# Six two-block sections for the input projection of a decoder layer, five of them with seven products

## The chip, the cores and the metric

The kernel runs on one core of a Trainium2 chip. TensorE multiplies matrices, VectorE (DVE) and ScalarE (ACT) work on tiles, GpSimd (POOL) and SyncE (SP) mostly issue DMAs; each engine takes its instructions in the order in which the program gives them. The metric is the device time in microseconds (us), the median of a few executions. Traces come from one further execution under the hardware profiler, and their times count from the start of its span.

## The reference

One decoder layer on 256 tokens of width 2048, in float32: attention with 16 heads of 128 and a bias table by distance, then a gated feed-forward network of width 5632, each followed by a residual and a layer norm. With 256 tokens there is only one key block, so the attention is plain causal attention. Cut to what is computed:

```python
q, k, v = split(x @ w_qkv, 3)                       # 256 x 2048 each, 16 heads
logits = (q * 128 ** -0.5) @ k.T + bias[t5_bucket(distance)]
p = softmax(where(key <= query, logits, -inf))
x1 = layer_norm(ALPHA * x + (p @ v) @ w_o)
y = layer_norm(ALPHA * x1 + (silu(x1 @ w_gate) * (x1 @ w_up)) @ w_down)
```

## The kernel before

Every large product runs in a split form: a float32 operand is written as a high part `hi` and a remainder `lo` in the format float32r (`split`, L82: a copy on ScalarE, a subtraction on VectorE), and a product takes three matmuls, hi x hi, hi x lo and lo x hi. A matmul has 512 columns and fills one of the eight PSUM banks.

The work is cut into sections (`Sec`, L86), each a few column blocks of 512 of a weight, over eight pairs of 128 input rows. The input projection has four sections q0 to q3, one for each group of four heads, with three column blocks: the group's q, k and v. Then come o0 and o1 (output projection), f0 to f10 (gate and up, one block each) and d (down). `alternate` (L179) lays out two blocks of matmuls for each pair, one for each half of the tokens: 18 matmuls a block in the input projection. The list `blocks` is the order of TensorE's work. Weights of pair p are loaded by SP's queue into one of six raw buffers and split a number of blocks ahead of the pair's first block (`start`, L212 to L221: three, `AHEAD`; in f1 to f10 six or five, `ST_AHEAD`).

The sections f1 to f10 use seven products for eight in the pairs 1, 3 and 5 (`ST`): the two halves of the tokens and the two column blocks form a 2 x 2 scheme over the two rows of a pair, `split_quad` (L240) forms four sums of weights and splits four operands, `combine` (L484) does the same for the input, `half_block` (L278) issues the products into seven banks, and `sums_mid`, `sums_gate` and `sums_up` (L550 to L579) put the results together again.

What else has to be done is hung on a block's number t: `before(t, ...)` ahead of the block's splits, `after(t, ...)` behind its matmuls. The main loop (L695) emits, for each t, the `before` entries, then the splits that are due, then the matmuls, then the `after` entries, and that is the order in every engine's queue. The attention of group g starts behind the first block after section g, one or two steps behind each block (`att_steps`): transposes of q and k of two heads a and b (`at_t1`), scores of a, scores of b with a's normalisation, b's normalisation with the transposes of a's probabilities (`at_t2`), those of b, and the two outputs (`at_o`). `at_s` (L344) also issues the evacuation of the scores on VectorE, the negated maximum `nm` and the exponentials on ScalarE. Banks come from a free list, first in, first out (`bank`, `give`). The second transposed `hn` of section f0 follows two blocks behind it (`gate_t`, L660).

Of the kernel before, what the change touches and what calls it, by code (L numbers as in the profile page):

```python
# [11 lines left out]
F = mybir.dt.float32  # L12
# [15 lines left out]
BIG = -3.0e38  # L28
RL = 384
# [8 lines left out]
ST_FROM = 1  # L38
# [9 lines left out]
def decoder_layer(ctx: ExitStack, tc: tile.TileContext, x, xt, rel_bias, w_qkv, w_o, g1, b1, gb1,  # L48
# [37 lines left out]
    class Sec:  # L86
        def __init__(self, name, chunks, npair, lhs):
            self.name, self.chunks, self.npair, self.lhs = name, chunks, npair, lhs
# [40 lines left out]
    def make_bias():  # L129
        pb = bank("pb")  # L130
        nc.tensor.matmul(pb[:H, :RL], tab, hot, start=True, stop=True)
        rs = const.tile([H, RL], F, name="rs")
        nc.vector.tensor_tensor(rs, pb[:H, :RL], msk, op=OP.add)
        give(pb)
        nc.gpsimd.dma_start(rows, rs)

    def load_bias(g):
# [4 lines left out]
        bias_t[g] = t  # L142

# [11 lines left out]
    x1T, x1D, x1C, x1f = {}, {}, [], {}  # L155
# [14 lines left out]
    FU = [Sec(f"f{i}", [(w_gate, i), (w_up, i)], 8, x1_lhs) for i in range(NF)]  # L170
# [27 lines left out]
    halved = {s.name for s in FU[ST_FROM:]}  # L198
# [72 lines left out]
    def d_lhs(kt):  # L271
        hi, lo = x1D[kt // 8]
        return hi[:, kt % 8, :], lo[:, kt % 8, :]

    def e_lhs(n):
        return x1C[0][:, n, :], x1C[1][:, n, :]

    def half_block(s, p, half):  # L278
        a, b = 2 * p, 2 * p + 1
        if p in ST:  # L280
            w = s.pieces[p, 0]
            n = 2 * ST.index(p)
            lhs = {1: x1_lhs(a, 0), 2: x1_lhs(b, 0), 3: e_lhs(n + 1), 5: e_lhs(n), 7: d_lhs(a),
                   6: d_lhs(b), 4: x1_lhs(b, 1)}
            for n in ((1, 2, 3), (7, 5, 6, 4))[half]:
                product(s, n, lhs[n], w[n], p == ST[-1] and n in (1, 6, 7))
        else:
            hi, lo = s.pieces[p, half]
            for k in range(2):
                kt = a + k  # L290
                w = hi[:, k, :], lo[:, k, :]
                for n, lhs in ((2, x1_lhs(kt, 0)), (4, x1_lhs(kt, 1))) if half == 0 else ((5, x1_lhs(kt, 1)), (3, d_lhs(kt))):
                    product(s, n, lhs, w, p == s.npair - 1 and k == 1)

    def block(s, pairs, m, chunks, ks):
        if s.name in halved:
# [20 lines left out]
    SC = HD ** -0.5  # L317
# [26 lines left out]
    def at_s(h):  # L344
# [139 lines left out]
    def combine(c):  # L484
        if c == 0:
            x1C.extend([p4([P, 8, P], R, "xeh"), p4([P, 8, P], R, "xel")])
        if c % 2 == 0:
            x1D[c // 2] = (p4([P, 8, P], R, "xdh"), p4([P, 8, P], R, "xdl"))
        t0, t1 = (x1f.pop((m, c)) for m in range(2))
        d = s2([P, CW], F, "xd")  # L490
        nc.vector.tensor_tensor(d, t0, t1, op=OP.subtract)
        col = lambda t, k: t[:, k * P:(k + 1) * P]
        for p in (2 * c, 2 * c + 1):
            if p not in ST:
                continue
            a, b = 2 * (p % 2), 2 * (p % 2) + 1
            e = s2([P, 2, P], F, "xe")
            nc.vector.tensor_tensor(col(d, b), col(d, a), col(t1, b), op=OP.add)
            nc.vector.tensor_tensor(e[:, 0, :], col(t1, a), col(t1, b), op=OP.subtract)
            nc.vector.tensor_tensor(e[:, 1, :], col(t0, b), col(d, b), op=OP.subtract)  # L500
            n = 2 * ST.index(p)
            split(x1C[0][:, n:n + 2, :], x1C[1][:, n:n + 2, :], e)
        hi, lo = x1D[c // 2]
# [257 lines left out]
```

## Time and profile before

| | us |
|---|---|
| median of 3 runs | 1125.44 (1125.1 to 1128.34) |
| profiled execution, its own time | 1128.58 |
| its span | 1126.8 |
| TensorE busy | 1108.4 (98%) |
| VectorE busy | 789.2 (70%) |
| ScalarE busy | 552.4 (49%) |
| first matmul of the projection, first of o0 | 4.68, 298.76 |
| DMA | 232.81 MB, mean 207 GB/s |

A busy TensorE is not one at its peak, since the ends of matmuls are modelled and overlap the next; the distance between the starts of two matmuls is their cost. PE is TensorE, PEld its weight loads. "Idle before" names what released an engine after a wait.

### The profile page before, as it was taken

To read this page: it belongs to the slowest core of one execution; us is meant where nothing else is said; L and a number is where in the kernel's file an instruction comes from. 1 tells how busy PE (TensorE), PEld (TensorE's weight loads), DVE (VectorE), ACT (ScalarE), POOL (GpSimd) and SP (SyncE) were. 2 spreads that over 40 slices of the span, in tenths; PEclk is the share of its full clock that TensorE was granted. 3 is DMA by queue.
4 is the path that set the end of the run, shared out by engine and by line. 5 is a ranking of instruction groups with operands and counts; after the bars stand their busy time and mean duration, and the time that the engine had idled before them with its cause. 6 is when DMAs were issued, how large, how long until landed. Compare 5 with 4: busy or idle time off the path is not lost.

```text
span 1126.8 us, 13508 instructions
## 1 busy us (share of the span) xinstructions
PE 1108.4 (98%) x5049; PEld 915.1 (81%) x5049; DVE 789.2 (70%) x1011; ACT 552.4 (49%) x700; POOL 10.3 (1%) x16
## 2 busy tenths in 40 slices
PE   9999999999999999999999999999999999999995
PEld 6888888888888887788888888888888888888884
DVE  7635555564568668888988988988988646664446
ACT  6534444444455456555655655655656534354320
POOL 0000000000000000000000000000000000000001
PEclk9999999999999999899999999999999999999998
DMA  9845555554466636746656646647649584587611
GB/s 330 323 145 175 165 178 185 180 181 154 155 226 200 255 107 219 275 131 236 228 168 240 222 169 244 222 162 251 217 183 339 181 334 184 196 308 261 224 38 75
DMA packets 65890, 232.81 MB, mean 207 GB/s; under 512 B 7520, under 2 KB 7968, under 8 KB 65824
## 3 DMA queue, kind: packets, MB, share of 16 engines
q1 hardware_dynamic: 63344, 223.01, 56.6%
q10 hardware_dynamic: 1872, 6.82, 1.5%
q0 software_dynamic: 608, 2.12, 0.6%
q8 instruction: 39, 0.64, 0.2%
q14 instruction: 27, 0.22, 0.1%
HBM read 222.98 MB, written 8.94 MB: 206 GB/s over the span
## 4 chain that ended last, share of the span: by engine, by line
PE 94%; DVE 3%; ACT 2%; issue 1%; DMA 0%; SPq 0%; POOL 0%; ACTq 0%; POOLq 0%; DVEq 0%
PE acc_f L267 12%; PE acc_f L269 12%; PE acc_f L268 12%; PE acc_q L310 8%; PE acc_q L314 8%; PE acc_q L311 8%; PE acc_d L311 7%; PE acc_d L310 7%; PE acc_d L314 7%; PE acc_o L310 2%; PE acc_o L311 2%; PE acc_o L314 2%; PE ov L396 1%; PE lg L351 1%; PE ht L587 1%
## 5 line engine op out<-in xcount | busy, mean ns | idle before, releaser
L84 DVE TENSOR_TENSOR wl_d<-r_d,wh_d 128x1024 fp32r<-128x1024 f32 x88 | 104.5, 1221 | 72.0 <-ACT wh_d L83 51.9
L310 PE MATMUL acc_q<-wh_q,xh 128*128 128x512 f32 x372 | 148.7, 400 | 0.0
L84 DVE TENSOR_TENSOR wl_f<-r_f,wh_f 128x1024 fp32r<-128x1024 f32 x116 | 135.0, 1218 | 17.5 <-ACT wh_f L83 17.5
L311 PE MATMUL acc_q<-wl_q,xh 128*128 128x512 f32 x372 | 145.3, 391 | 0.0
L310 PE MATMUL acc_d<-wh_d,hh 128*128 128x512 f32 x352 | 137.0, 389 | 0.0
L311 PE MATMUL acc_d<-wl_d,hh 128*128 128x512 f32 x352 | 136.9, 389 | 0.0
L83 ACT ACTIVATE wh_d<-r_d 128x1024 fp32r<-128x1024 f32 x88 | 91.0, 1058 | 76.1 <-DMA r_d<-in_w_down 48.8
L84 DVE TENSOR_TENSOR wl_q<-r_q,wh_q 128x1024 fp32r<-128x1024 f32 x93 | 109.3, 1220 | 26.4 <-ACT wh_q L83 25.7
L83 ACT ACTIVATE wh_f<-r_f 128x1024 fp32r<-128x1024 f32 x116 | 115.7, 1049 | 11.2 <-DMA r_f<-in_w_up 4.5
L267 PE MATMUL acc_f<-wh_f,x1h 128*128 128x512 f32 x300 | 116.8, 389 | 0.0
L269 PE MATMUL acc_f<-wh_f,x1l 128*128 128x512 f32 x300 | 116.7, 389 | 0.0
L268 PE MATMUL acc_f<-wl_f,x1h 128*128 128x512 f32 x300 | 116.7, 389 | 0.0
L314 PE MATMUL acc_q<-wh_q,xl 128*128 128x512 f32 x372 | 105.0, 390 | 0.0
L83 ACT ACTIVATE wh_q<-r_q 128x1024 fp32r<-128x1024 f32 x93 | 93.3, 1053 | 17.2 <-DMA r_q<-in_w_qkv 17.2
L314 PE MATMUL acc_d<-wh_d,hl 128*128 128x512 f32 x352 | 99.9, 389 | 0.0
L314 PEld LDWEIGHTS acc_q<-wh_q,xl 128*128 128x128 f32 x372 | 69.8, 188 | 15.0
L310 PEld LDWEIGHTS acc_q<-wh_q,xh 128*128 128x128 f32 x372 | 70.0, 188 | 14.0 <-issue 0.6
L311 PEld LDWEIGHTS acc_q<-wl_q,xh 128*128 128x128 f32 x372 | 70.0, 188 | 13.2
L83 ACT ACTIVATE aq<-t 128x1024 fp32r<-128x1024 f32 x30 | 31.9, 1063 | 94.7 <-DVE t L247 94.7
L310 PEld LDWEIGHTS acc_d<-wh_d,hh 128*128 128x128 f32 x352 | 66.1, 188 | 13.8
L314 PEld LDWEIGHTS acc_d<-wh_d,hl 128*128 128x128 f32 x352 | 66.1, 188 | 13.7
L311 PEld LDWEIGHTS acc_d<-wl_d,hh 128*128 128x128 f32 x352 | 66.1, 188 | 13.7
(185 smaller groups left out, 1946.5 us busy)
## 6 DMA issues: line engine op xcount, KB each, us to landing
r_q<-in_w_qkv SPq DMA_DIRECT2D x93, 512.0 KB, 4.8
r_f<-in_w_gate SPq DMA_DIRECT2D x88, 512.0 KB, 3.7
r_f<-in_w_up SPq DMA_DIRECT2D x88, 512.0 KB, 5.0
r_d<-in_w_down SPq DMA_DIRECT2D x88, 512.0 KB, 5.9
r_o<-in_w_o SPq DMA_DIRECT2D x32, 512.0 KB, 4.3
hd<-hT ACTq DMA_DIRECT2D x9, 512.0 KB, 6.7
hT<-hd SPq DMA_DIRECT2D x9, 512.0 KB, 3.6
bias<-rows POOLq DMA_DIRECT2D x4, 512.0 KB, 7.4
```

The costliest lines, as they stand in the source:

```text
L83: nc.scalar.activation(hi, src, AF.Copy)
L84: nc.vector.tensor_tensor(lo, src, f32(hi), op=OP.subtract)
L267: nc.tensor.matmul(a, lh, rh, start=start, stop=False)
L268: nc.tensor.matmul(a, lh, rl, start=False, stop=False)
L269: nc.tensor.matmul(a, ll, rh, start=False, stop=stop)
L310: nc.tensor.matmul(a, lh, hi[:, k, :], start=kt == 0, stop=False)
L311: nc.tensor.matmul(a, lh, lo[:, k, :], start=False, stop=False)
L314: nc.tensor.matmul(s.acc[m, c], ll, hi[:, k, :], start=False, stop=kt == nk - 1)
L351: nc.tensor.matmul(b[:, o:o + n], a[:, qs], c[:, ks], start=i == 0, stop=i == 2)
L396: nc.tensor.matmul(b[:, o:o + w], a[:, m, js], c[:, ks:ks + w], start=n == 0, stop=n == 5)
L587: nc.tensor.transpose(out=b[:, j * P:(j + 1) * P], in_=t[:, j * P:(j + 1) * P], identity=ident)
```

## The change

The input projection becomes six sections of two column blocks: q and k of group 0, v of groups 0 and 1, q and k of group 1, q and k of group 2, v of groups 2 and 3, q and k of group 3. All but the first use seven products in the pairs 1, 3 and 5, with the code of the gate/up sections made general; their splits are issued three blocks ahead, those of q0 five. `combine_x` forms the combined input pair by pair behind the blocks of q0. Results are put together in three steps at the end of a section (`sums_1` to `sums_3`), shared with gate/up. Blocks now have 12 matmuls (9 in the first block of a seven-product pair), and seven banks are taken, so attention has one spare.

Attention of groups 0 to 3 runs in q2, q3, q5 and o0. Values stay in float32 and are split per head in `at_t2`; the scale moves into the exponentials; the normalisation moves from VectorE to ScalarE; the outputs of groups 0 to 2 are evacuated unsplit, stored to DRAM, loaded again and split ahead of o0. The second `hn` of f0 is transposed four blocks behind the section instead of two.

```diff
+SC = HD ** -0.5
-ST_FROM = 1
+AHEAD_Q = 5
+QKV = (((0, 0), (1, 0)), ((2, 0), (2, 1)), ((0, 1), (1, 1)), ((0, 2), (1, 2)), ((2, 2), (2, 3)), ((0, 3), (1, 3)))
+SQK, SV = {0: 0, 1: 2, 2: 3, 3: 5}, {1: (0, 1), 4: (2, 3)}
...
-        nc.vector.tensor_tensor(rs, pb[:H, :RL], msk, op=OP.add)
+        nc.vector.scalar_tensor_tensor(rs, pb[:H, :RL], 1.0 / SC, msk, op0=OP.mult, op1=OP.add)
...
+    def combine_x(p):
+        r = x_raw[p]
+        combine(xC, 2 * p, r[:, :, :P], r[:, :, P:], "x")
...
-    Q = [Sec(f"q{g}", [(w_qkv, 4 * i + g) for i in range(3)], 8, x_lhs) for g in range(4)]
+    xC, x1C = {}, {}
+    Q = [Sec(f"q{n}", [(w_qkv, 4 * i + g) for i, g in pair], 8, x_lhs, xC if n else None)
+         for n, pair in enumerate(QKV)]
...
+    for p in range(1, 8):
+        start["q0", p] = first["q0", p] - AHEAD_Q
...
-    for s in FU[ST_FROM:]:
+    for s in [*Q[1:], *FU[1:]]:
         for p in range(s.npair):
-            start[s.name, p] = first[s.name, p] - ST_AHEAD[p in ST]
+            start[s.name, p] = first[s.name, p] - (AHEAD if s in Q else ST_AHEAD[p in ST])
...
+    def combine(comb, kt, t0, t1, name):
+        n = t0.shape[1]
+        d = s2([P, n, P], F, name + "d")
+        nc.vector.tensor_tensor(d, t0, t1, op=OP.subtract)
+        for p in range(kt // 2, (kt + n) // 2):
+            if p not in ST:
+                continue
+            a = 2 * p - kt
+            b = a + 1
+            e = s2([P, 2, P], F, name + "e")
+            nc.vector.tensor_tensor(d[:, b, :], d[:, a, :], t1[:, b, :], op=OP.add)
+            nc.vector.tensor_tensor(e[:, 0, :], t1[:, a, :], t1[:, b, :], op=OP.subtract)
+            nc.vector.tensor_tensor(e[:, 1, :], t0[:, b, :], d[:, b, :], op=OP.subtract)
+            if "e" not in comb:
+                comb["e"] = (p4([P, 8, P], R, name + "eh"), p4([P, 8, P], R, name + "el"))
+            i = 2 * ST.index(p)
+            split(*(v[:, i:i + 2, :] for v in comb["e"]), e)
+        if kt // 8 not in comb:
+            comb[kt // 8] = (p4([P, 8, P], R, name + "dh"), p4([P, 8, P], R, name + "dl"))
+        i = kt % 8
+        split(*(v[:, i:i + n, :] for v in comb[kt // 8]), d)
...
-    def qkv_evac(g, m):
-        s = Q[g]
-        if m == 0:
-            grp[g] = (p4([P, 2, CW], F, f"qn{g}"), p4([P, 2, CW], F, f"kn{g}"),
-                      p4([P, 2, CW], R, f"vh{g}"), p4([P, 2, CW], R, f"vl{g}"))
-        qn, kn, vh, vl = grp[g]
-        nc.scalar.activation(qn[:, m, :], s.acc[m, 0], AF.Copy, scale=SC)
-        nc.vector.tensor_copy(kn[:, m, :], s.acc[m, 1])
-        split(vh[:, m, :], vl[:, m, :], s.acc[m, 2])
-        give(*(s.acc[m, c] for c in range(3)))
+    def new_qk(g):
+        grp[g] = {n: p4([P, 2, CW], F, f"{n}{g}") for n in "qk"}
+        return grp[g]
+    def first_qk(m):
+        t = new_qk(0) if m == 0 else grp[0]
+        nc.scalar.activation(t["q"][:, m, :], Q[0].acc[m, 0], AF.Copy)
+        nc.vector.tensor_copy(t["k"][:, m, :], Q[0].acc[m, 1])
+        give(Q[0].acc[m, 0], Q[0].acc[m, 1])
+    def sums_1(s, t):
+        a = s.acc
+        nc.scalar.activation(t[0], a[1], AF.Copy)
+        nc.vector.tensor_tensor(t[2], t[0], a[6], op=OP.subtract)
+        nc.vector.tensor_tensor(t[3], t[2], a[7], op=OP.add)
+        give(a[1], a[6], a[7])
+    def sums_2(s, t):
+        a = s.acc
+        nc.vector.tensor_tensor(t[0], t[0], a[2], op=OP.add)
+        nc.vector.tensor_tensor(t[1], t[3], a[4], op=OP.add)
+        give(a[2], a[4])
+    def sums_3(s, t):
+        a = s.acc
+        nc.vector.tensor_tensor(t[2], a[5], t[2], op=OP.subtract)
+        nc.vector.tensor_tensor(t[3], a[5], t[3], op=OP.subtract)
+        nc.vector.tensor_tensor(t[2], a[3], t[2], op=OP.add)
+        give(a[5], a[3])
+    sums = {}
+    def qk_sums(g, step):
+        s = Q[SQK[g]]
+        if step == 1:
+            t = new_qk(g)
+            sums[s.name] = [t["q"][:, 0, :], t["q"][:, 1, :], t["k"][:, 0, :], t["k"][:, 1, :]]
+        (sums_1, sums_2, sums_3)[step - 1](s, sums[s.name])
+    def v_sums(n, step):
+        s = Q[n]
+        if step == 1:
+            for g in SV[n]:
+                grp[g, "v"] = p4([P, 2, CW], F, f"v{g}")
+            sums[s.name] = [grp[g, "v"][:, m, :] for g in SV[n] for m in range(2)]
+        (sums_1, sums_2, sums_3)[step - 1](s, sums[s.name])
...
-        nc.vector.tensor_scalar(nm, mx, -1.0, None, op0=OP.mult)
+        nc.vector.tensor_scalar(nm, mx, -SC, None, op0=OP.mult)
...
-        nc.scalar.activation(sc[:, :2 * P], sc[:, :2 * P], AF.Exp, bias=nm[:, 0:1], accum_out=sm[:, 0:1])
-        nc.scalar.activation(sc[:, 2 * P:], sc[:, 2 * P:], AF.Exp, bias=nm[:, 1:2], accum_out=sm[:, 1:2])
+        nc.scalar.activation(sc[:, :2 * P], sc[:, :2 * P], AF.Exp, scale=SC, bias=nm[:, 0:1], accum_out=sm[:, 0:1])
+        nc.scalar.activation(sc[:, 2 * P:], sc[:, 2 * P:], AF.Exp, scale=SC, bias=nm[:, 1:2], accum_out=sm[:, 1:2])
...
-        nc.vector.tensor_scalar(sc[:, :2 * P], sc[:, :2 * P], rs[:, 0:1], None, op0=OP.mult)
-        nc.vector.tensor_scalar(sc[:, 2 * P:], sc[:, 2 * P:], rs[:, 1:2], None, op0=OP.mult)
+        nc.scalar.activation(sc[:, :2 * P], sc[:, :2 * P], AF.Identity, scale=rs[:, 0:1])
+        nc.scalar.activation(sc[:, 2 * P:], sc[:, 2 * P:], AF.Identity, scale=rs[:, 1:2])
...
-        att[h] = [hi, lo]
+        vs = [s2([P, 2, P], R, f"v{i}") for i in "hl"]
+        split(*vs, grp[h // 4, "v"][:, :, h % 4 * P:(h % 4 + 1) * P])
+        att[h] = [hi, lo, *vs]
...
+        if g == 3:
+            oh, ol = oT[g]
+            split(oh[:, j, :], ol[:, j, :], b[:, :S])
+        else:
+            nc.scalar.activation(oT[g][:, j, :], b[:, :S], AF.Copy)
+            if j == 3:
+                nc.scalar.dma_start(od[g], oT.pop(g))
         give(b)
+    def load_o(g):
+        oT[g] = p4([P, 4, S], F, f"o{g}")
+        nc.sync.dma_start(oT[g], od[g])
+    def split_o(g):
+        t = oT[g]
+        oT[g] = (p4([P, 4, S], R, f"oh{g}"), p4([P, 4, S], R, f"ol{g}"))
+        split(*oT[g], t)
...
-    after(6, load_small)
-    after(9, make_bias)
+    after(9, load_small)
+    after(13, make_bias)
+    for p in range(8):
+        after(2 * p + 4, combine_x, p)
+    def at_sums(s, f, *a):
+        t = last[s.name, 1]
+        after(first[s.name, ST[-1]] + 1, f, *a, 1)
+        after(t - 1, f, *a, 2)
+        after(t, f, *a, 3)
+    for m in range(2):
+        after(last["q0", m], first_qk, m)
+    for n in SV:
+        at_sums(Q[n], v_sums, n)
     for g in range(4):
-        after(10 if g < 2 else last[f"q{g - 1}", 1], load_bias, g)
-        for m in range(2):
-            after(last[f"q{g}", m], qkv_evac, g, m)
-        t0 = last[f"q{g}", 1] + 1
+        if g:
+            at_sums(Q[SQK[g]], qk_sums, g)
+        t0 = (first["q2", 0], first["q3", 0], first["q5", 0], first["o0", 0])[g]
+        before(t0 - 3, load_bias, g)
         for n, step in enumerate(att_steps(g)):
             for f, h in step:
                 after(t0 + n, f, h)
+        if g < 3:
+            after(first["o0", 2 * g] - 5, load_o, g)
+            after(first["o0", 2 * g] - 3, split_o, g)
...
-            after(min(t + (m + 1 if i < ST_FROM else 2 + m), first["d", 1]), gate_t, i, m)
+            after(min(t + (2 + m if i else 1 + 3 * m), first["d", 1]), gate_t, i, m)
...
-    for c in range(3):
+    for c in range(2):
...
```

`half_block`, `d_lhs` and `e_lhs` take the section's own operands; otherwise they are as before.

## Rows read from the trace of the kernel before

**Rows 1.** the profile's page, busy time, share and instructions by engine

```profile
PE 1108.4 (98%) x5049; PEld 915.1 (81%) x5049; DVE 789.2 (70%) x1011; ACT 552.4 (49%) x700; POOL 10.3 (1%) x16
```

**Rows 2.** the page, chain that ended last, shares by engine

```profile
PE 94%; DVE 3%; ACT 2%; issue 1%; DMA 0%; SPq 0%; POOL 0%; ACTq 0%; POOLq 0%; DVEq 0%
```

**Rows 3.** two stretches: us, busy (count) by engine, granted clock, DMA, GB/s

```profile
75.00:149.00 74.00, 74.00 (x360) 61.76 (x360) 42.69 (x76) 34.00 (x55) 0.75 (x1) 1.00 0.55 178
487.00:530.00 43.00, 43.00 (x195) 35.62 (x194) 37.37 (x44) 23.45 (x27) 0.00 (x0) 1.00 0.62 210
```

**Rows 4.** timeline, VectorE, behind the first gate/up section: start us, us, what [idle before]

```profile
443.49 0.68 DVE L246 TENSOR_TENSOR t<-r_f,r_f 128x512 f32<-128x512 f32 x1
...
446.02 1.22 DVE L84 TENSOR_TENSOR gq<-r_f,gq 128x1024 fp32r<-128x1024 f32 x1
...
450.03 2.35 DVE L84 TENSOR_TENSOR wl_f<-r_f,wh_f 128x1024 fp32r<-128x1024 f32 x2
452.30 0.68 DVE L544 TENSOR_TENSOR hn<-acc_f,sg 128x512 f32<-128x512 f32 x1
```

**Rows 5.** timeline, TensorE, the same stretch

```profile
449.34 0.39 PE L269 MATMUL acc_f<-wh_f,xdl 128*128 128x512 f32 x1
453.03 1.11 PE L587 MATMUL ht<-ident,hn 128*128 128x128 f32 x4 [3.30 <-DVE hn L544]
453.80 0.78 PE L267 MATMUL acc_f<-gq,x1h 128*128 128x512 f32 x1
...
459.07 0.43 PE L267 MATMUL acc_f<-aq,xeh 128*128 128x512 f32 x1
```

**Rows 6.** stretch behind that wait, columns as in Rows 3

```profile
453.00:456.00 3.00, 2.97 (x9) 2.57 (x10) 2.96 (x5) 1.46 (x2) 0.00 (x0) 0.50 0.84 288
```

**Rows 7.** timeline, TensorE, nine matmuls of section q0

```profile
17.18 0.39 PE L310 MATMUL acc_q<-wh_q,xh 128*128 128x512 f32 x1
...
19.22 0.39 PE L310 MATMUL acc_q<-wh_q,xh 128*128 128x512 f32 x1
```

**Rows 8.** timeline, TensorE, q1: first instruction of attention steps, each behind an 18-matmul block

```profile
83.91 0.38 PE L338 MATMUL t<-ident,qn 128*128 128x128 f32 x2
...
88.46 0.28 PE L351 MATMUL lg<-qkh 128*128 128x256 f32 x1
...
93.27 0.28 PE L351 MATMUL lg<-qkh 128*128 128x256 f32 x1
...
98.09 0.49 PE L379 MATMUL t<-ident,sc 128*128 128x128 f32 x3
102.54 0.49 PE L379 MATMUL t<-ident,sc 128*128 128x128 f32 x3
```

**Rows 9.** groups by line: what, count, busy us, mean ns, idle before

```profile
L84 DVE TENSOR_TENSOR ol<-ov,oh 128x256 fp32r<-128x256 f32 x16 | 6.8, 424 | 29.3 <-ACT oh L83 29.3
L372 DVE TENSOR_SCALAR sc<-sc,rs 128x256 f32<-128x256 f32 x16 | 5.7, 354 | 0.6
```

**Rows 10.** timeline, VectorE, q1: evacuation of two heads' scores

```profile
89.30 0.42 DVE L355 CUSTOM_DVE_ANT_0 sc<-lg,bias 128x256 f32<-128x256 f32 x1 [3.42 <-PE lg L351]
...
95.56 0.42 DVE L355 CUSTOM_DVE_ANT_0 sc<-lg,bias 128x256 f32<-128x256 f32 x1
...
96.23 0.17 DVE L361 TENSOR_SCALAR nm<-mx 128x2 f32<-128x2 f32 x1
```

**Rows 11.** timeline, ScalarE, q1: one head's exponentials

```profile
96.43 0.51 ACT L363 ACTIVATE sc<-sc,nm 128x256 f32<-128x256 f32 x1 [2.42 <-DVE nm L361]
...
96.94 0.39 ACT L364 ACTIVATE sc<-sc,nm 128x128 f32<-128x128 f32 x1
97.23 0.19 ACT L364 ACTIVATION_READ_ACCUMULATOR sc<-sc,nm 128x1 f32 x1
```

**Rows 12.** the page, DMA issues: count, KB each, us to landing

```profile
hd<-hT ACTq DMA_DIRECT2D x9, 512.0 KB, 6.7
...
bias<-rows POOLq DMA_DIRECT2D x4, 512.0 KB, 7.4
```

More of the change, by code (lines that the diff above doesn't have):

```diff
@@ L86, in decoder_layer, with __init__ @@
     class Sec:
[L87 to L88 removed]
+        def __init__(self, name, chunks, npair, lhs, comb=None):
+            self.name, self.chunks, self.npair, self.lhs, self.comb = name, chunks, npair, lhs, comb
             self.acc = {}
@@ L269, in product, with d_lhs, e_lhs @@
         nc.tensor.matmul(a, ll, rh, start=False, stop=stop)
[L271 to L276, printed above, removed]
+    def combine(comb, kt, t0, t1, name):
[19 more added lines that the diff above has]
+        split(*(v[:, i:i + n, :] for v in comb[kt // 8]), d)
+    def d_lhs(s, kt):
+        return tuple(v[:, kt % 8, :] for v in s.comb[kt // 8])
+    def e_lhs(s, n):
+        return tuple(v[:, n, :] for v in s.comb["e"])
     def half_block(s, p, half):
@@ L291, in half_block @@
                 w = hi[:, k, :], lo[:, k, :]
-                for n, lhs in ((2, x1_lhs(kt, 0)), (4, x1_lhs(kt, 1))) if half == 0 else ((5, x1_lhs(kt, 1)), (3, d_lhs(kt))):
+                for n, lhs in ((2, s.lhs(kt, 0)), (4, s.lhs(kt, 1))) if half == 0 else ((5, s.lhs(kt, 1)), (3, d_lhs(s, kt))):
                     product(s, n, lhs, w, p == s.npair - 1 and k == 1)
     def block(s, pairs, m, chunks, ks):
-        if s.name in halved:
+        if s.comb is not None:
             half_block(s, pairs[0], m)
@@ L395, in at_o @@
             for a, c in ((vh, hi), (vh, lo), (vl, hi)):
-                nc.tensor.matmul(b[:, o:o + w], a[:, m, js], c[:, ks:ks + w], start=n == 0, stop=n == 5)
+                nc.tensor.matmul(b[:, o:o + w], a[:, m, :], c[:, ks:ks + w], start=n == 0, stop=n == 5)
                 n += 1
-        oh, ol = oT[g]
-        split(oh[:, j, :], ol[:, j, :], b[:, :S])
-        give(b)
+        if g == 3:
[5 more added lines that the diff above has]
+                nc.scalar.dma_start(od[g], oT.pop(g))
+        give(b)
+    def load_o(g):
[5 more added lines that the diff above has]
+        split(*oT[g], t)
     def att_steps(g):
@@ L482, in ln1_t, with combine_x1 @@
         split(hi[:, a:a + 4, :], lo[:, a:a + 4, :], t.rearrange("p (j c) -> p j c", j=4))
[L484 to L503, printed above, removed]
-        n = 4 * (c % 2)
-        split(hi[:, n:n + 4, :], lo[:, n:n + 4, :], d.rearrange("p (j c) -> p j c", j=4))
+    def combine_x1(c):
+        t0, t1 = (x1f.pop((m, c)).rearrange("p (j c) -> p j c", j=4) for m in range(2))
+        combine(x1C, 4 * c, t0, t1, "x1")
     def ln1_affine(m, c):
@@ L640, in decoder_layer @@
     for c in range(4):
-        after(f0_t[1][0] + (1, 2, 4, 6)[c], combine, c)
+        after(f0_t[1][0] + (1, 2, 4, 6)[c], combine_x1, c)
     after(f0_t[0][3], store_y, 0)
@@ L655, in decoder_layer @@
         else:
-            after(first[f"f{i}", ST[-1]] + 1, sums_mid, i)
-            after(t - 1, sums_gate, i)
-            after(t, sums_up, i)
+            at_sums(FU[i], gate_sums, i)
         for m in range(2):
-            after(min(t + (m + 1 if i < ST_FROM else 2 + m), first["d", 1]), gate_t, i, m)
+            after(min(t + (2 + m if i else 1 + 3 * m), first["d", 1]), gate_t, i, m)
     after(dn_t[0][0] - 10, load_ln, g2, b2, "ln2")
@@ L685, in decoder_layer @@
         load_x(0, slice(k, k + 1))
-        for c in range(3):
+        for c in range(2):
             r, src = s.raws[0, c]
@@ L690, in decoder_layer @@
         split_x(0, slice(k, k + 1))
-        for c in range(3):
+        for c in range(2):
             hi, lo = s.pieces[0, c]
@@ L702, in decoder_layer @@
                 split_x(p, slice(0, 2))
-            if ss.name in halved and p in ST:
+            if ss.comb is not None and p in ST:
                 split_quad(ss, p)
```

63 lines of the change are left out of this document (22 added, 41 removed).

## The prediction

> **What bounds the kernel now.** I read the engine shares first, then the chain of waits, then the busy time by stretch. TensorE is busy 98% of the span [rows 1] and carries 94% of the chain that ended last [rows 2], so a matmul removed is time removed as long as TensorE stays fed. VectorE is the next engine: 42.69 of 74 us in an attention section of the input projection, 37.37 of 43 us in a section of the gate/up stage, which already works with seven products [rows 3]. TensorE was busy throughout both stretches. So VectorE at 87% of a stretch does no harm by itself; the order of its queue has to be looked at as well.
>
> One place shows that. Behind the first gate/up section, the second `hn` (L544) waits on VectorE behind the seven-product split of the next section and a plain split: the seven-product split runs from 443.49 to 450.03 (6.54 us), the plain one to 452.30 (2.27 us), and only then does `hn` start [rows 4]. TensorE's last matmul before the wait starts at 449.34; the transposes of `hn` start at 453.03 [rows 5]. With 0.23 us for that last matmul TensorE stood for 3.46 us. Behind the wait the granted clock is 0.50 (1.2 of 2.4 GHz) [rows 6]; twelve matmuls take from 453.80 to 459.07 [rows 5].
>
> **What is removed.** Nine matmuls start between 17.18 and 19.22 [rows 7]: 0.2267 us each. A seven-product pair needs 21 matmuls for 24. Five sections with three such pairs: 45 fewer, 45 x 0.2267 = 10.2 us. All are on the path.
>
> The Trainium skill ("TensorE: Matmul & The Clock Gate", Back-to-back issue gap) gives about 131 ns for a sustained matmul of 512 columns; by it the edit would save 5.9 us, and the sum below would be 4.3 us higher. The pitch of this kernel's own matmuls is 227 ns, so I go by that.
>
> The second `hn` transposes move from two blocks behind the first gate/up section to four. The wait of 3.46 us goes, and with it the slow clock: twelve matmuls at full pitch are 2.72 us instead of 5.27, and four transposes 0.47 [rows 8] instead of 0.77; together 2.9. What is late next: in block 3 of that section product 7 takes the seventh bank of the free list, which is one that the same `hn` reads until 452.98 [rows 4]. Block 3 would start at 449.57 + 9 x 0.2267 = 451.6, so 1.4 us remain. Gain 3.46 + 2.9 - 1.4 = 5.0 us (between 0, if the short wait also lowers the clock and costs what the long one did, and 6.4).
>
> **What VectorE gets.** Fifteen seven-product splits for plain ones: 15 x (6.54 - 2.27) = 64 us. Sums: 7 x 0.63 (four adds from 443.49 to 446.02 [rows 4]) = 4.4 us in each of five sections, 22 us, where about 9 us of evacuation go. Values split per head: 16 x 0.42 [rows 9] = 7 us. Combining `x`: 16 such operations and a few small ones, 11 us. The two normalising operations, 0.35 and about 0.28, leave for ScalarE: -10 us [rows 9]. Net about 83 us over the projection, nearly all in five sections. An attention section then has 3 x 6.54 + 5 x 2.27 + 4.4 + about 12 = 47 us of VectorE against 183 x 0.2267 + 9.2 = 50.7 us of TensorE (9.2: four heads at 0.47, 0.73, 0.37 and 0.73, each the distance of two rows less the 4.08 of 18 matmuls [rows 8]). By the average it fits; sections q1 and q4, without attention, have 35 against 41.5 and I cost them at nothing: nothing in them waits for TensorE before block 11, so VectorE runs ahead.
>
> **Where the order bites.** Splits are issued three blocks ahead, so pair 3's seven-product split stands in VectorE's queue between head a's scores (behind block 2) and head b's scores and a's normalisation (behind block 3); the transposes of a's probabilities come behind block 4. From the first score matmul of a: score evacuation starts after 0.84 us and takes 0.84 to the end of `nm` [rows 8, 10], 1.7; split 6.54, 8.2; b's scores 0.84, 9.0. ScalarE then does b's exponentials, 0.99 from 96.43 to 97.42 [rows 11], 10.0, and only then a's normalisation, priced by the same two tiles there, 0.42 + 0.39, 10.8. TensorE arrives after 0.73 + 2.72 (block 3) + 0.73 + 2.72 (block 4) = 6.9 us. It waits **3.9 us**. In the kernel before, the same place held a plain split, blocks took 4.08 us and a's normalisation did not follow b's exponentials, and a's transposes (98.09) came 4.82 us behind b's scores (93.27) [rows 8], that is one block and the scores themselves, with no wait.
>
> In q2 and q5 VectorE is late before that. From the end of the last block but one of the section before: two sums 1.2, split of pair 1 6.5, three sums 1.8, a's q and k 0.6, plain split 2.3, b's q and k 0.6, with 0.2 to start: 13.2 us. TensorE has finished a's scores after 2.72 + 2.72 + 0.47 + 2.72 + 0.47 + 2.04 + 0.73 = 11.9. So 1.3 more: **5.2 us** in each. In q3 the heads' q and k are q2's own sums, which stand behind q3's pair 1: 0.2 + 1.2 + 6.54 + 1.8 = 9.75 us against 0.73 + 2.72 + 0.73 + 2.72 = 6.9: **2.9 us** at the first transposes, then 3.9. The second pair of heads meets plain splits there, and waits under 0.2 us. Together 5.2 + 2.9 + 3.9 + 5.2 = **17.2 us** (bounds: 0, if something starts these splits earlier; 22, if each normalisation and each transition is 1 us later).
>
> Three of the four waits are longer than the 3.46 us after which the clock is seen to fall: 3 x 2.9 = **8.7 us**. The fourth I count at nothing (0 to 2.9). The Trainium skill (same page, Part 1) reports 6 to 14 slow matmuls for one kernel from run to run; at 0.21 us each, three falls would by that cost 3.8 to 8.8 us. Here twelve were slow.
>
> **Costed at nothing.** ScalarE's extra splits, exponent scale and normalisations: it is busy 34 of 74 us [rows 3]; the order effect is counted above. Combining `x` lies beside q0's blocks, which wait for no such operation before q1; if it were in the way, the first section would lose up to its 11 us. The spill of three outputs: a store lands 6.7 us after its issue [rows 12]; the reload of group 2 stops SP's queue until then, with the pieces for o0's pair 4 behind it, whose use is 13 us further on. The bias load on POOL's queue is issued five blocks (13.6 us) ahead of use and lands in 7.4 [rows 12]. Four chunks instead of six before the first matmuls: 0, within 1 either way. One spare bank: its turns wait for the same VectorE operations as counted.
>
> **The sum.** -10.2 - 5.0 + 17.2 + 8.7 = +10.7 us. The profiled execution took 1128.58 us (span 1126.8), so 1139.3 for such a one. It lies 3.1 above the median of the three runs, 1125.44, and the new time is a median too: **1136 us**.
>
> **Rivals.** (A) VectorE keeps up: the splits start early enough that nothing waits. For: 47 against 50.7 us, and gate/up sections at 87% without waits. Against: head a's scores stand before the split, so it can't start before TensorE is through block 2; the gate/up sections issue six blocks ahead, these three. Then only the gains count, 1125.4 - 15.2 = 1110: faster. (B) The waits come, but the clock stays up or the waits shrink by as much: 1125.4 + 17.2 - 15.2 = 1127.4, the same. For: the only fall seen had transposes around it; against: rows 6. (C) More of it: the fourth wait lowers the clock too and the mended place gains nothing: 1136 + 2.9 + 5.0 = 1144. The point that decides between A and the forecast is whether a's probabilities are normalised within 6.9 us of a's scores.
>
> **How the numbers follow.** The forecast 0.54, C 0.08, B 0.2, A 0.18 (which may end anywhere from 1110 to 1121, as part of the waits stays). About 0.3% (3.4 us) is what a measurement can tell here. Faster 0.18, same 0.2, slower 0.62. The forecast's own range is 1130 to 1142; to leave out no more than 2 in 10, the range goes from 1117, inside A, to 1144.
>
> **What would show it.** Right: in q2, q3 and q5 TensorE idle for 4 to 5 us in front of the first probability transposes, released by ScalarE's normalisation, with VectorE busy on a seven-product split just before; one wait of about 3 us at the start of q3's attention on VectorE's sums; granted clock 0.50 behind them; no 3.46 us wait behind the first gate/up section. Wrong: the projection from first matmul to o0 in 284 us or less with TensorE unbroken (A), or waits with matmuls still 0.23 us apart behind them (B).

## The result and the profile after

The changed kernel takes **1145.48 us** (1144.72 to 1146.3, 4 runs) against 1125.27 for the kernel before beside it: ratio 1.0174, 95% interval 1.0154 to 1.0194, slower by some 20 us. The forecast was 1136, slower by some 11, and its range ended at 1144: the side was right, the forecast size was half of the measured one, and the time lies 1.5 us above the range. The profiled execution took 1146.3 (span 1144.5), 17.7 more than the profiled one of before.

From the page of after, busy time by engine and the chain that ended last, the lines that answer to [rows 1] and [rows 2]:

```profile
PE 1105.3 (97%) x5004; PEld 908.7 (79%) x5004; DVE 867.8 (76%) x1124; ACT 591.5 (52%) x782; POOL 10.3 (1%) x16
PE 82%; DVE 10%; ACT 4%; issue 2%; DMA 1%; SPq 0%; POOL 0%; ACTq 0%; DVEq 0%; POOLq 0%
```

The 45 matmuls are gone, but TensorE's part of the chain fell from 94% to 82%: VectorE and ScalarE now decide 14% of the way.

The first matmul of each stage shows where the time went. From the first matmul of the projection to that of o0 it is 313.3 us (before 294.1), +19.2; o0 and o1 take 99.2, +1.8; gate/up takes 474.8, -3.5; the rest is within 0.3. The answer to [rows 3], two stretches of after (columns as there):

```profile
118.00:160.00 42.00, 37.23 (x186) 30.58 (x185) 30.94 (x52) 21.26 (x39) 0.76 (x1) 0.98 0.47 156
500.00:540.00 40.00, 40.00 (x182) 33.09 (x181) 35.76 (x42) 23.27 (x27) 0.00 (x0) 1.00 0.62 208
```

In the attention section TensorE idles for nearly 5 of 42 us although VectorE is busy for only 31 of them; in the gate/up stage VectorE is busier and TensorE never stops.

TensorE's waits in after, grouped by what ended them (total us, times, longest us):

```profile
PE t L447 <- ACT sc L441: 16.9, 6, 4.3
PE t L406 <- DVE k L379: 4.7, 2, 3.9
PE ht L631 <- ACT hT L632: 2.5, 1, 2.5
```

L447 transposes the probabilities, L441 is the normalisation on ScalarE, L406 transposes q and k, L379 is the last of the sums. A row shows some 0.16 us less than TensorE stood, as the last matmul's modelled end lies behind its pitch of 0.23; below, waits are counted from that pitch. In the projection they are 4.45 (q2), 1.66, 4.07 and 3.84 (q3), 1.72, 4.43 (q5) and 1.73: 21.9 us. The first one, TensorE in q2:

```profile
109.35 0.39 PE L280 MATMUL acc_q<-wh_q,xl 128*128 128x512 f32 x1
114.03 0.90 PE L447 MATMUL t<-ident,sc 128*128 128x128 f32 x3 [4.29 <-ACT sc L441]
114.58 0.77 PE L278 MATMUL acc_q<-wh_q,xh 128*128 128x512 f32 x1
...
118.99 0.55 PE L279 MATMUL acc_q<-wl_q,xdh 128*128 128x512 f32 x1
```

VectorE and ScalarE in the same stretch:

```profile
110.29 1.22 DVE L87 TENSOR_TENSOR bq<-t,bq 128x1024 fp32r<-128x1024 f32 x1
111.42 0.42 DVE L423 CUSTOM_DVE_ANT_0 sc<-lg,bias 128x256 f32<-128x256 f32 x1
```
```profile
112.30 0.51 ACT L431 ACTIVATE sc<-sc,nm 128x256 f32<-128x256 f32 x1 [2.94 <-DVE nm L429]
...
113.59 0.39 ACT L441 ACTIVATE sc<-sc,rs 128x128 f32<-128x128 f32 x1
```

The last piece of the seven-product split, then b's scores, b's exponentials, then a's normalisation, and only then the transposes: the forecast's chain, step by step. Behind the wait the matmuls stand 0.43 us apart instead of 0.23, at this granted clock (columns as in [rows 3], the clock behind the busy times):

```profile
114.00:118.00 4.00, 3.97 (x11) 3.29 (x12) 2.15 (x4) 3.35 (x6) 0.00 (x0) 0.50 0.01 4
```

That is half of the 2.4 GHz level. Behind the four long waits of the projection 11, 6, 11 and 7 matmuls are slow and lose 7.5 us together; behind the three short ones none is. So the projection's 19.2 us are -10.2 (matmuls) + 21.9 (waits) + 7.5 (clock). The start and the slow transposes, each under 2 us, are not separated, so it is partly luck that the sum closes exactly.

### The profile page after: what moved, and what is told of

Read it like the earlier page. It is cut to its first block, busy times and chain, and to the rows that moved or that the text cites. A ratio compares the mean times of both kernels' runs of the same rounds, so it can differ in the third digit from the quotient of the medians.

```text
span 1144.5 us, 13666 instructions
## 1 busy us (share of the span) xinstructions
PE 1105.3 (97%) x5004; PEld 908.7 (79%) x5004; DVE 867.8 (76%) x1124; ACT 591.5 (52%) x782; POOL 10.3 (1%) x16
## 4 chain that ended last, share of the span: by engine, by line
PE 82%; DVE 10%; ACT 4%; issue 2%; DMA 1%; SPq 0%; POOL 0%; ACTq 0%; DVEq 0%; POOLq 0%
PE acc_f L278 12%; PE acc_f L280 12%; PE acc_f L279 12%; PE acc_d L342 7%; PE acc_d L343 7%; PE acc_d L346 7%; PE acc_q L278 4%; PE acc_q L280 4%; PE acc_q L279 4%; PE acc_o L342 2%; PE acc_o L343 2%; PE acc_o L346 2%; PE acc_q L343 1%; PE acc_q L346 1%; PE acc_q L342 1%
## 5 line engine op out<-in xcount | busy, mean ns | idle before, releaser
L86 ACT ACTIVATE aq<-t 128x1024 fp32r<-128x1024 f32 x45 | 47.7, 1060 | 124.5 <-DVE t L258 114.6
L87 DVE TENSOR_TENSOR wl_q<-r_q,wh_q 128x1024 fp32r<-128x1024 f32 x64 | 75.6, 1221 | 12.4 <-ACT wh_q L86 11.9
L86 ACT ACTIVATE wh_q<-r_q 128x1024 fp32r<-128x1024 f32 x64 | 64.1, 1048 | 3.3 <-DMA r_q<-in_w_qkv 2.9
L280 PEld LDWEIGHTS acc_f<-wh_f,x1l 128*128 128x128 f32 x300 | 56.3, 188 | 11.8
L278 PEld LDWEIGHTS acc_f<-wh_f,x1h 128*128 128x128 f32 x300 | 56.3, 188 | 11.6
L279 PEld LDWEIGHTS acc_f<-wl_f,x1h 128*128 128x128 f32 x300 | 56.3, 188 | 11.6
L278 PE MATMUL acc_q<-wh_q,xh 128*128 128x512 f32 x150 | 62.7, 418 | 0.0
L280 PE MATMUL acc_q<-wh_q,xl 128*128 128x512 f32 x150 | 60.2, 401 | 0.0
L279 PE MATMUL acc_q<-wl_q,xh 128*128 128x512 f32 x150 | 59.9, 399 | 0.0
```

Source lines behind the costliest of these rows:

```text
L86: nc.scalar.activation(hi, src, AF.Copy)
L87: nc.vector.tensor_tensor(lo, src, f32(hi), op=OP.subtract)
L278: nc.tensor.matmul(a, lh, rh, start=start, stop=False)
L279: nc.tensor.matmul(a, lh, rl, start=False, stop=False)
L280: nc.tensor.matmul(a, ll, rh, start=False, stop=stop)
```

## Experiments

The leading theory (ORDER): the waits come from what stands ahead in the queues of VectorE and ScalarE. The rival (VOLUME): VectorE has too much to do. All edits are against the changed kernel unless another is named, all ratios against the kernel before on the same chip.

### 1. The attention of the first three groups one block later

```diff
-                after(t0 + n, f, h)
+                after(t0 + n + (g < 3), f, h)
```

> The changed kernel with the attention of groups 0 to 2 one block later against the splits, nothing else. Theory ORDER (TensorE waits because attention operations stand behind a split in the queues of VectorE and ScalarE): the seven-product split of pair 3 then stands before head a's scores instead of behind them; the first waits shrink from 4.3 to about 1.7 us, the second ones (1.7) go, the wait on q3's sums falls from 4.1 to about 1, and no wait is long enough for the slow clock: 1123 us, between 1119 and 1129. Rival VOLUME (VectorE has too much work in an attention section, 47 of 51 us): the work is the same, 1142 to 1147 us.

Measured 1146.96 (1144.9 to 1148.12), ratio 1.0195 (1.0180 to 1.0210): nothing gained, and inside VOLUME's range, not ORDER's. TensorE in q2:

```profile
110.58 0.43 PE L419 MATMUL lg<-qkh 128*128 128x256 f32 x1 [2.45 <-DVE mx L425]
...
120.11 0.55 PE L447 MATMUL t<-ident,sc 128*128 128x128 f32 x3 [1.85 <-DVE ptl L87]
```

The one long wait became two short ones: b's score matmuls wait for the one spare bank, which a's evacuation (L425), now behind the split, still holds, and a later step meets the next split. The waits moved with the order, but the time didn't: with seven-product splits this frequent, a shift by a block only moves the collision. By the time alone this run speaks for VOLUME; it is experiment 3 that parts the two.

### 2. a's normalisation right behind a's scores

```diff
-            one = [[(at_t1, a)], [(at_t1, b)], [(at_s, a)], [(at_s, b), (at_n, a)],
+            one = [[(at_t1, a)], [(at_t1, b)], [(at_s, a), (at_n, a)], [(at_s, b)],
```

> The changed kernel with the normalisation of head a issued right behind its own scores instead of behind head b's. It is then done before the transposes need it. If the place of the normalisation alone makes the wait, the six waits in front of probability transposes go, and with them the slow clock: 1121 to 1126 us. If the one spare bank is as late (head b's scores are evacuated behind the split too), the first waits stay at 3.5 to 4 us and the second ones at about 1: 1141 us, 1137 to 1144.

Measured 1145.22 (1144.97 to 1145.27), ratio 1.0181 (1.0166 to 1.0196). TensorE, then VectorE in q2:

```profile
113.12 0.52 PE L447 MATMUL t<-ident,sc 128*128 128x128 f32 x3 [3.91 <-DVE mx L425]
```
```profile
111.20 1.22 DVE L87 TENSOR_TENSOR bq<-t,bq 128x1024 fp32r<-128x1024 f32 x1
112.34 0.42 DVE L423 CUSTOM_DVE_ANT_0 sc<-lg,bias 128x256 f32<-128x256 f32 x1
```

a is normalised long before (by 106.8 us), and the wait stays: its releaser is now the evacuation of b's scores, whose bank the transposes need. So the place of the normalisation alone was not the point that decides; the spare bank behind the split is as late. The time lies 1.2 us above the range put for this; in the second pairs the transposes of b's probabilities now wait too, 1.1 us three times.

### 3. The normalisation back on VectorE

```diff
-        nc.scalar.activation(sc[:, :2 * P], sc[:, :2 * P], AF.Identity, scale=rs[:, 0:1])
+        nc.vector.tensor_scalar(sc[:, :2 * P], sc[:, :2 * P], rs[:, 0:1], None, op0=OP.mult)
```

(and the same for the second part)

> The changed kernel with the normalisation back on VectorE. ORDER: a's normalisation no longer stands behind b's exponentials on ScalarE, each of the six waits gets about 0.85 us shorter: 1139 us, 1136 to 1142. VOLUME: VectorE gets 10 us more work, so 1147 to 1155 us.

Measured **1134.46** (1134.38 to 1135.6), ratio 1.0085 (1.0069 to 1.0102): 11 us faster with more on VectorE. That refutes VOLUME as it was put. ORDER's 1139 was 4.5 us too high: the waits before the probability transposes shrank by the 0.85 us each that it counted, and beside them the wait on q3's sums fell from 4.07 to 2.98 and o0's loss of 1.8 went. TensorE in q2, first and second pair of heads:

```profile
112.26 0.90 PE L447 MATMUL t<-ident,sc 128*128 128x128 f32 x3 [3.45 <-DVE sc L441]
139.51 0.55 PE L447 MATMUL t<-ident,sc 128*128 128x128 f32 x3 [0.65 <-DVE sc L441]
```

The waits are 4.29 and 1.50 in after. On ScalarE a's normalisation comes behind b's exponentials; on VectorE it runs beside them.

### 4. Seven products in two pairs instead of three in q2, q3 and q5

```diff
+            self.st = (1, 5) if name in ("q2", "q3", "q5") else ST
-        if p in ST:
+        if p in s.st:
```

Pair 3 is then formed from an operand that is not the plain difference, so the sums of these sections differ; the work is that of a plain pair.

> The changed kernel with seven products in pairs 1 and 5 only in q2, q3 and q5 (nine matmuls more, 2.0 us). ORDER: a plain split stands in the critical place, the first waits fall from 4.3 to about 1.7 us like the second ones, and the slow clock behind them goes: 1132 us, 1128 to 1136. VOLUME: 13 us less for VectorE, which would give at most those 13 us less the 2: 1134 to 1140. A weak separation; it prices the pair.

Measured 1138.69 (1137.87 to 1140.1), ratio 1.0125 (1.0109 to 1.0140). That is inside VOLUME's range and 2.7 us above ORDER's, whose centre was 6 us too low; the run does not speak against VOLUME. The first pair of heads in q2 and q5 still waits 2.28, the sums 4.06, and the clock falls behind both kinds. Counted by the trace: 9 matmuls +2.0, waits -6.5, slow matmuls -1.9 make -6.4; measured -6.8 (-7.6 between the profiled executions).

### 5. The seven-product split in two parts, a block apart

```diff
-        split(*a2, t13)
-        split(*b2, t24)
+        def rest():
...
+            split(*a2, t13)
+            split(*b2, t24)
+        rest() if late is None else before(late, rest)
```

> The changed kernel with each seven-product split of the projection issued in two parts, one block apart (two adds and three operands first, then two adds and the other operands); the same instructions, 3.0 and 3.5 us of VectorE instead of 6.5 in one piece. ORDER: b's scores and a's normalisation no longer stand behind 6.5 us, the first waits fall from 4.3 to about 0.5, the wait on q3's sums from 4.1 to nothing, the slow clock goes, the second waits (1.7) stay: 1122 us, 1118 to 1130. VOLUME: the same work and the same waits in other places, as it was when attention was moved by one block: 1142 to 1147 us.

Measured 1139.54 (1138.36 to 1140.03), ratio 1.0123 (1.0109 to 1.0137). TensorE in q2:

```profile
110.62 0.55 PE L454 MATMUL t<-ident,sc 128*128 128x128 f32 x3 [1.75 <-ACT sc L448]
116.10 0.55 PE L454 MATMUL t<-ident,sc 128*128 128x128 f32 x3 [2.19 <-DVE ptl L87]
```

The wait on q3's sums is down to 0.5, and a's wait nearly to what the second pair has (1.7); but b's transposes now meet the other half. The time lies between the two ranges: ORDER's size was wrong again.

### 6. Experiments 3 and 5 together, with two steps more

Beside both edits, a's transposes go ahead of b's normalisation, and the second `hn` transposes five blocks behind f0:

```diff
-            after(min(t + (2 + m if i else 1 + 3 * m), first["d", 1]), gate_t, i, m)
+            after(min(t + (2 + m if i else 1 + 4 * m), first["d", 1]), gate_t, i, m)
```

> As the run with two parts, with the normalisation on VectorE, a's transposes in front of b's normalisation, and the second hn of the first gate/up section transposed five blocks behind it. ORDER: the second waits fall to 0.8, the 3.1 us in front of hn go: 1114 us, 1110 to 1120, faster than both kernels. VOLUME: 10 us more for VectorE, 1130 to 1140 us, not below the kernel before.

Measured 1127.83 (1126.05 to 1129.6, 10 runs), ratio 1.0021 (1.0012 to 1.0030). That is 14 us above ORDER's 1114, though below VOLUME's range. No wait is left behind f0, but eleven in the projection are, 0.7 to 2.3 us each, 14 us together.

### 7. No seven products in the projection

Six plain sections (45 matmuls back), with four spare banks instead of one:

```diff
-    Q = [Sec(f"q{n}", [(w_qkv, 4 * i + g) for i, g in pair], 8, x_lhs, xC if n else None)
+    Q = [Sec(f"q{n}", [(w_qkv, 4 * i + g) for i, g in pair], 8, x_lhs)
```

> The changed kernel without the seven products in the projection (six plain sections of two blocks, four spare banks, no combining of x). 45 matmuls more, 10.2 us. If only the seven-product splits make the waits: no wait left, 1122 to 1127 us. If blocks of 2.72 us instead of 4.08 are themselves too short for the chain of scores, exponentials, a plain split, scores, exponentials and normalisation: all six pairs of heads wait 1.7 us as the second pairs do, 1135 us, 1131 to 1139.

Measured 1134.87 (1133.86 to 1135.26), ratio 1.0082 (1.0068 to 1.0095). TensorE in q2:

```profile
113.70 0.55 PE L456 MATMUL t<-ident,sc 128*128 128x128 f32 x3 [1.50 <-ACT sc L450]
```

There are six such waits, 1.65 or 1.72 each, with no seven-product split in the projection: some 10 us come from the two-column sections and the place of the normalisation, as the second reading had it. The fifteen seven-product pairs as placed, with the three banks that they take, make it 10.6 us worse, though they save 10.2 of matmuls.

### 8. The kernel before, with the later hn alone

```diff
-            after(min(t + (m + 1 if i < ST_FROM else 2 + m), first["d", 1]), gate_t, i, m)
+            after(min(t + (1 + 3 * m if i < ST_FROM else 2 + m), first["d", 1]), gate_t, i, m)
```

> The kernel before with the second hn of the first gate/up section transposed four blocks behind it instead of two, nothing else. By the stage of the two traces (478.2 and 474.8 us) the edit saves 3.5 us where the clock falls behind the old wait. If the clock falls there in some runs of the kernel before and not in others (its runs lie near 1125 and near 1128): 1124 to 1125 us, with the spread gone. If it falls in all: 1122 us.

Measured 1124.78 (1122.92 to 1125.4, 11 runs), ratio 0.9989 (0.9980 to 0.9998). The edit is worth 0.6 us in the median; no run came near 1128, but the runs lie near 1123.3 and near 1125.1, so a spread remains. It goes with the granted clock: its mean over the span is 0.996 in the runs near 1123.3 and 0.994 or 0.995 in the others. The trace still has a wait of 2.67 us before the second `hn` transposes, with slow matmuls behind it; why the mean clock differs from run to run stays open.

### 9. Seven products only in q1 and q4, where no attention runs

Plain sections as in experiment 7 for the others, with the normalisation on VectorE and `hn` five blocks behind f0:

```diff
-    Q = [Sec(f"q{n}", [(w_qkv, 4 * i + g) for i, g in pair], 8, x_lhs, xC if n else None)
+    Q = [Sec(f"q{n}", [(w_qkv, 4 * i + g) for i, g in pair], 8, x_lhs, xC if n in SV else None)
```

> Seven products stay only in q1 and q4, the two sections that no attention runs beside; q0, q2, q3 and q5 are plain sections of two column blocks. Besides, the normalisation is back on VectorE and the second hn of the first gate/up section is transposed five blocks behind it. Counted from the form without seven products in the projection (1134.87): 18 matmuls fewer, 18 x 0.2267 = -4.1; the 2.5 us wait behind the first gate/up section goes; six waits on the normalisation shrink from 1.5 to 0.65, -5.1. ORDER theory (a seven-product split costs only where attention steps stand behind it in VectorE's queue): 1123 us (1120 to 1127), TensorE unbroken through q1 and q4. Rival VOLUME (each seven-product pair costs VectorE time that is missing later, as the 15 pairs cost 10.6 us net): 6 x 0.7 = +4.2 instead of -4.1, 1131 us (1128 to 1134), with waits at the starts of q2 and q5.

Measured **1122.29** (1121.73 to 1122.93, 8 runs), ratio 0.9977 (0.9967 to 0.9987): where ORDER put it. TensorE waits six times on the normalisation, 0.89 us each (0.74 in the rows), and nowhere in q1 or q4.

### 10 and 11. An extra block before a's probabilities, with and without those pairs

Both against experiment 9; the second is without seven products in q1 and q4 too.

```diff
-            one = [[(at_t1, a)], [(at_t1, b)], [(at_s, a)], [(at_s, b), (at_n, a)],
-                   [(at_n, b), (at_t2, a)], [(at_t2, b)], [(at_o, a)], [(at_o, b)]]
+            one = [[(at_t1, a), (at_t1, b)], [(at_s, a)], [(at_s, b)], [(at_n, a)],
+                   [(at_t2, a), (at_n, b)], [(at_t2, b)], [(at_o, a)], [(at_o, b)]]
```

> As the kernel with seven products in q1 and q4 alone, and the attention steps spaced anew: both heads' q and k are transposed behind one block, and one block more stands between the scores of head b and the transposes of a's probabilities. ORDER theory (the 0.65 us left before a's probability transposes is the chain scores, plain split, normalisation against two 2.72 us blocks): with a third block that wait goes everywhere, -0.7 x 6 = 4 us against that kernel: 1119 us (1116 to 1123). Rival (what is gained there is lost at the front: with both transposes behind one block, head a's score matmuls come behind VectorE's plain split, 2.3, and two operand splits in less than 3.2 us): waits of 0.5 to 1 us at the first score matmuls instead, time as without the edit, 1123 us (1121 to 1126).

> No seven products in the projection at all, with the other three edits of the kernel with the spaced steps (normalisation on VectorE, second hn five blocks behind, the extra block before a's probabilities). What it tells: what the six seven-product pairs of q1 and q4 are worth by themselves. ORDER: they are worth their 18 matmuls, so this kernel is 4.1 us slower than the one with them, 1123 us (1120 to 1127). Rival VOLUME: they cost as much as they save or more, so this one is as fast or up to 4 us faster.

Measured 1122.38 (1122.06 to 1122.58, 11 runs; ratio 0.9977, 0.9968 to 0.9986) and 1126.59 (1125.48 to 1127.22, 11 runs; ratio 1.0011, 1.0002 to 1.0020). The difference, 4.2 us, is the 18 matmuls (4.1): the pairs in q1 and q4 are worth all that they save. The extra block gained nothing, and not for the rival's reason either, since no score matmul waits. Experiment 10 in q2, second pair of heads, TensorE, then VectorE, then ScalarE:

```profile
137.91 0.52 PE L447 MATMUL t<-ident,sc 128*128 128x128 f32 x3 [0.79 <-DVE sc L441]
```
```profile
134.54 2.36 DVE L87 TENSOR_TENSOR wl_q<-r_q,wh_q 128x1024 fp32r<-128x1024 f32 x2 [2.06 <-ACT wh_q L86]
136.82 0.16 DVE L438 TENSOR_SCALAR rs<-sm 128x2 f32<-128x2 f32 x1
...
137.49 0.28 DVE L441 TENSOR_SCALAR sc<-sc,rs 128x128 f32<-128x128 f32 x1
```
```profile
132.57 0.51 ACT L431 ACTIVATE sc<-sc,nm 128x256 f32<-128x256 f32 x1 [1.97 <-DVE nm L429]
...
133.46 1.99 ACT L86 ACTIVATE wh_q<-r_q 128x1024 fp32r<-128x1024 f32 x2
```

The normalisation stands behind a plain split whose VectorE half is idle for 2.06 us, because its ScalarE half is queued behind b's exponentials. The operands of the normalisation had been ready all that time: a's exponentials end at 130.6 us.

### 12. Both normalisations ahead of that split

Against experiment 10:

```diff
-            one = [[(at_t1, a), (at_t1, b)], [(at_s, a)], [(at_s, b)], [(at_n, a)],
-                   [(at_t2, a), (at_n, b)], [(at_t2, b)], [(at_o, a)], [(at_o, b)]]
+            one = [[(at_t1, a), (at_t1, b)], [(at_s, a)], [(at_s, b), (at_n, a), (at_n, b)], [(at_t2, a)],
+                   [(at_t2, b)], [(at_o, a)], [(at_o, b)], []]
```

> As the kernel with seven products in q1 and q4 alone, with another order of the attention steps: both heads' q and k are transposed behind one block, the scores of a one block later, then, behind the same block, the scores of b and both heads' normalisations, and a block later each the transposes of the probabilities. ORDER theory (what was left of the waits, 0.75 us six times, was a normalisation behind a plain split whose VectorE half stands idle, 2.06 us from 132.48 to 134.54 in the kernel with the extra block, because its ScalarE half is queued behind the exponentials): with the normalisations ahead of that split they run inside its idle time, nothing waits, and six waits of 0.75 us go: 1122.3 - 4.5 = 1118 us (1116 to 1120). Rival (the waits aren't on the path, since TensorE makes them up at the next bank or transfer): 1122 us (1121 to 1123). Second rival (b's normalisation, which needs b's exponentials, holds up the split behind it, and product blocks wait for weights): 1122 to 1126 us.

Measured **1116.45** (1116.17 to 1117.06, 5 runs), ratio 0.9924 (0.9910 to 0.9937): faster than both kernels. The page's busy time and chain, then TensorE in q2 at the second pair of heads, and VectorE there:

```profile
PE 1099.6 (99%) x5031; PEld 908.7 (82%) x5031; DVE 830.5 (75%) x1087; ACT 567.4 (51%) x735; POOL 10.3 (1%) x16
PE 94%; DVE 2%; ACT 1%; DMA 1%; issue 1%; SPq 0%; POOL 0%; ACTq 0%; POOLq 0%; DVEq 0%
```
```profile
133.16 0.49 PE L447 MATMUL t<-ident,sc 128*128 128x128 f32 x3
```
```profile
131.96 0.28 DVE L441 TENSOR_SCALAR sc<-sc,rs 128x128 f32<-128x128 f32 x1
...
133.18 0.28 DVE L441 TENSOR_SCALAR sc<-sc,rs 128x128 f32<-128x128 f32 x1
133.46 2.36 DVE L87 TENSOR_TENSOR wl_q<-r_q,wh_q 128x1024 fp32r<-128x1024 f32 x2
```

Both normalisations run in what was the idle time, and no wait of TensorE over 0.2 us is left in q1 to o1, although a's transposes come a block earlier behind b's scores than in experiment 10: the order gained what the distance had not. Against the profiled execution of before, gate/up is 6.2 us shorter, about what the wait and the low clock behind f0 took [rows 5, 6], and the projection 5.8, of which 4.1 are the 18 matmuls; that execution lay 3.1 above the median of its kernel, so the medians differ by less, 8.7. TensorE does 27 matmuls more than in after, and the kernel is 29 us faster.

## Why the prediction was half right

The mechanism held at the first pairs of heads and at q3's sums; the sum came out 9.5 us low, by the terms below.

**The matmuls, -10.2**, and **the waits of the first pair of heads** held: mechanism, place and releaser as put; 4.45, 3.84 and 4.43 us against 5.2, 3.9 and 5.2.

**The second pair of heads, "waits under 0.2 us there": the step that failed most.** It waits 1.66, 1.72 and 1.73, 5.1 us in all. VectorE, then ScalarE, then TensorE in after:

```profile
138.31 2.36 DVE L87 TENSOR_TENSOR wl_q<-r_q,wh_q 128x1024 fp32r<-128x1024 f32 x2 [2.00 <-ACT wh_q L86]
140.59 0.42 DVE L423 CUSTOM_DVE_ANT_0 sc<-lg,bias 128x256 f32<-128x256 f32 x1
```
```profile
137.24 2.00 ACT L86 ACTIVATE wh_q<-r_q 128x1024 fp32r<-128x1024 f32 x2
...
142.76 0.39 ACT L441 ACTIVATE sc<-sc,rs 128x128 f32<-128x128 f32 x1
```
```profile
143.20 0.55 PE L447 MATMUL t<-ident,sc 128*128 128x128 f32 x3 [1.50 <-ACT sc L441]
```

I had priced a plain split at its 2.27 us of VectorE. It costs 4.3, as its first half waits on ScalarE behind the exponentials that follow a's scores. The chain comes to 8.6 us against 6.9 on TensorE. In the kernel before, that hop stood in the trace too, but a block took 4.08 us:

```profile
92.15 3.50 DVE L84 TENSOR_TENSOR wl_q<-r_q,wh_q 128x1024 fp32r<-128x1024 f32 x3 [2.00 <-ACT wh_q L83]
```

Experiments 3, 7 and 12 show what makes this wait: with the normalisation on VectorE 0.81 remain (0.65 in the row), without seven products in the projection nothing changes, and with the order of experiment 12 all of it goes.

**The sums of q3, 2.9**: 4.07. What delayed the second pair also held back what stands ahead of them: the first step of q2's sums found VectorE idle behind a copy that follows a's normalisation on ScalarE.

```profile
143.66 0.69 DVE L365 TENSOR_TENSOR k<-q,acc_q 128x512 f32<-128x512 f32 x1 [1.96 <-ACT q L364]
```

With the normalisation on VectorE (experiment 3) it is 2.98, as forecast.

**The low clock, 8.7**: 7.5. It fell behind all four long waits, also the one that I had counted at nothing, but over 6 to 11 matmuls, not twelve each time. The Trainium skill ("TensorE: Matmul & The Clock Gate", Part 1) reports 6, 11 or 14 slow matmuls at the start of one kernel from run to run; here, behind waits in the middle of one execution, there were 11, 6, 11 and 7.

**The hn behind f0, -5.0**: -3.5. The bank that I named as late next did not hold up product 7. Another did: the second transposes take the bank of the first, whose evacuation stands on ScalarE behind the next split's copies. TensorE and ScalarE in after:

```profile
475.49 0.40 PE L280 MATMUL acc_f<-bq,x1l 128*128 128x512 f32 x1
478.40 0.66 PE L631 MATMUL ht<-ident,hn 128*128 128x128 f32 x4 [2.51 <-ACT hT L632]
```
```profile
475.42 1.06 ACT L86 ACTIVATE aq<-t 128x1024 fp32r<-128x1024 f32 x1 [3.18 <-DVE t L258]
476.81 1.06 ACT L86 ACTIVATE bq<-t 128x1024 fp32r<-128x1024 f32 x1 [0.33 <-DVE t L260]
477.77 0.58 ACT L632 ACTIVATE hT<-ht 128x512 f32<-128x512 f32 x1
```

One block more (experiments 6, 9 and 12) clears it.

**Costed at nothing**: the attention beside o0 lost 1.8, of which 1.4 are a wait of 0.94 on its group's sums and one of 0.45.

**From the profile to the median, -3.1**: after's profiled execution lies 0.8 above its median, so 2.3 of the miss are this step's. The runs of the kernel before lie between 1123.6 and 1128.3, and its profiled one was at the upper end.

Together, against the sum: waits +4.7, clock -1.2, hn +1.5, o0 +1.8, median +2.3: 9.1 of the 9.5 us. The net of 83 us for VectorE is a slip, its terms add up to 85; measured, its busy time grew by 78.6, and no other term hung on it. Rival C (1144) was right that the fourth wait lowers the clock too, but not that the mended place gains nothing, so that it came nearest is in part luck; A and B are out by the waits and by the low clock.

## What to carry to other kernels

An engine that is 76% busy, as VectorE is in after, can still hold up the one that bounds the kernel: list what stands ahead of each short, urgent step in its queue, and price a split over two engines as a chain through both queues, not by its half on one. When blocks are made shorter (4.08 to 2.72 us), every chain that was hidden behind two of them has to be worked out anew. Put the products that make long queue entries where nothing urgent shares the queue: 18 matmuls saved in q1 and q4 gave 4.2 us, the other 27 as placed cost 9.3 us more than they saved (experiments 3 and 9, less 2.9 for the later `hn`). Whether those 27 would pay with the order of experiment 12 was not tried.

## What the runs showed of the chip

The granted clock is not set by the length of the wait alone. After's wait of 2.68 us behind f0 left it up, and so did the same wait in experiments 1 to 5 and 7 (2.66 to 2.68); in experiment 8, 2.67 us, it fell. The stretches behind them, after and then experiment 8:

```profile
478.40:481.40 3.00, 3.00 (x15) 2.56 (x16) 3.00 (x4) 2.60 (x4) 0.00 (x0) 1.00 0.78 296
```
```profile
455.40:458.40 3.00, 3.00 (x11) 2.48 (x12) 3.00 (x3) 2.60 (x4) 0.00 (x0) 0.64 0.87 299
```

In the profiled executions of before, after and experiments 1 to 8, each of the 15 waits of 2.9 us and more was followed by slow matmuls (0.43 us, 5 to 12 of them), and of those between 1.8 and 2.7 us some were and some weren't. A forecast for this kernel can count on the low clock behind the long ones and take it as a chance behind the others; what decides there, no run shows.
